# Embedding products on a shared PSUM bank, the last token tiles, a partition maximum and the last stores: a hybrid encoder block on one core

## Chip, cores and metric

One core of one Trainium2 chip runs the whole program in one launch. The metric is the device time in microseconds (us) of that core; a profiled execution gives a span, from its first to its last instruction, and a trace. PE is TensorE, DVE VectorE, ACT ScalarE, POOL GpSimd, SP the engine whose queue issues most DMAs.

## What is computed

Two sequences (a prompt and a sample) of 2048 tokens with 1024 channels go through one encoder layer with shared weights:

```
z = rmsnorm(h) @ w_in                  # q | k | v | gate a | f | gate f
a  = softmax(q k^T / 8) v * silu(ga)   # 8 query heads, 2 key heads, width 64, rotary positions
fo = (Re FFT2(f) per group @ w_fmix) * silu(gf)
h  = h + concat(a, fo) @ w_out
h  = h + (p @ w_ple) * sigmoid(rmsnorm(h) @ w_ple_gate)
y  = rmsnorm(h)
```

## The kernel before

Matrices are split into a high and a low float16 half, and a product of two splits is three matmuls. The program has three parts.

**Projection.** `project` forms z tile by tile and stores q and k (`qTd`, `kTd`), v, gates and the first half of the transform in DRAM. A store made in one iteration is put in the list `stores_next` and issued at the start of the next iteration; what is left is issued in the last one, `i == n + 3`.

**Attention with a filler.** `attention` runs 64 units (sequence, key head, 128 queries) of 8 steps. A step puts on the PE the scores of two key tiles (`scores`, bank `ps_s`), the maxima of a later unit (`maxima`, `ps_m`, reduced on DVE as `a_mx`), and in some steps more: at step 4 of a unit the softmax sums of the unit before (`sums`), at step 6 the row maxima (`max_rows`, called from `turn`), at steps 0 and 4 the products with v (`pv`). ACT takes exponentials from `ps_s`, POOL adds them up (`acc`). Behind each step `interleave` lets a generator, the filler, write its own instructions for a share of the total `FILL`, in us as the code counts them; a filler that yields `None` ends its share of that step. PE, ACT, DVE and SP run in the order in which this code is written; POOL's order is set by the framework's scheduler.

The filler is first `fourier2`, the second half of the transform, and from its middle on `outp`: for each of 32 token tiles t, `out1` (product with w_out, two halves of the columns), then a norm, `out3` (the gate product) and the embedding's product, six matmuls, which close the tile. `mix` finds the scale that a sequence's tiles are split with, from a maximum over all partitions. A group of 24 full matmuls is done as 24 matmuls over the upper 64 rows of the array and 24 over the lower 64; `slot` holds a group back by one slot, so that `halves` writes the lower half of one group alternately with the upper half of the next, each pair side by side on the array.

Of the eight PSUM banks, scores, maxima and outputs take five; `ps_g` has two buffers (the groups of `outp`) and `ps_f` has **one**, the small bank. While `outp` runs, `bank()` hands out `ps_f` alone: to the sums (read by DVE's reciprocal and a multiplication), the row maxima (read by DVE as `mr`), and the embedding's products (read by DVE at L1405 and L1407). `defer` puts such a DVE operation into a list that `flush` issues at the start of the next step.

**Tail.** After the last attention step the bank pool `psX` opens with five banks, and the rest of `outp` runs without the attention and in the scheduler's order. From there on `slot` takes groups whole, 24 matmuls over 128 rows. A `seen` copy on DVE stands ahead of the lower half that is left over.

Of the kernel before, what the change touches and what calls it, by code (L numbers as in the profile page):

```python
# [29 lines left out]
CAP = 5.0  # L30
FILL = 775.0
AHEAD = 13
# [7 lines left out]
LAG = 3  # L40
P32 = 7
STOPS = (6, 9, 12, 15, 18)
MB = 2
# [96 lines left out]
class Build:  # L140
    def __init__(self, ctx, tc, a, y):
        self.ctx, self.tc, self.nc = ctx, tc, tc.nc
        self.a, self.y = a, y
        nc = self.nc
        ep = ctx.enter_context
        self.const = ep(tc.tile_pool(name="const", bufs=1))
        self.st = ep(tc.tile_pool(name="st", bufs=2))
        self.psF = ep(tc.tile_pool(name="psF", bufs=1, space=PSUM))
        self.psG = ep(tc.tile_pool(name="psG", bufs=2, space=PSUM))
        self.grouped = False  # L150
# [408 lines left out]
    def project(self, P, PU, W, early, wkv, wq, wga, bg, mid):  # L559
# [163 lines left out]
        def lo_q(i):  # L723
# [19 lines left out]
            stores_next.append(lambda: nc.sync.dma_start(self.kTd[s][:, :, c].rearrange("v p y r -> p v y r"), kT[:]))  # L743

# [33 lines left out]
        def iteration(i):  # L778
# [180 lines left out]
    def fourier2(self, pool, hook):  # L959
# [135 lines left out]
    def attention(self, kvp):  # L1095
# [88 lines left out]

        def max_rows(u):

            ps = self.bank()
            nc.tensor.matmul(ps[:, 0:128], nm[:], self.ident[:], start=True, stop=True)  # L1188
            MR[u] = mr = kvp.tile([128, 4, 128], F16, name="mr", bufs=1)
            nc.vector.tensor_tensor(out=mr[:], in0=ps[:, 0:128].unsqueeze(1).to_broadcast([128, 4, 128]),  # L1190
                                    in1=own[:].unsqueeze(2).to_broadcast([128, 4, 128]), op=ALU.mult)
# [36 lines left out]

        def sums(u):

            s, kv, t = units[u]
            acc, at = ACC.pop(u), AT.pop(u)
            av = acc[:, 0, :].rearrange("p (c e q) -> p e c q", e=2, q=128)
            ps = self.bank()
            for e in range(2):
                nc.tensor.matmul(ps[64 * e:64 * e + 64, 0:256], ones[:], av[:, e], start=True, stop=True)  # L1236
            r, x = ps[:, 256:512], at[:].rearrange("p c q -> p (c q)")
            nc.vector.reciprocal(r, ps[:, 0:256])  # L1238
            nc.vector.tensor_tensor(out=x, in0=x, in1=r, op=ALU.mult)
# [25 lines left out]

        def turn(g):
            v, k = divmod(g + 2, 8)
            if k == 0 and 0 <= v < n:
                max_rows(v)

        def leads():
            for g in range(-AHEAD, 0):
                yield from lead(g)
                yield
                turn(g)

        self.ahead = leads()
        pool = yield 0.0
        ones = pool.tile([128, 64], F32, name="ones", bufs=1)
        nc.gpsimd.memset(ones[:], 1.0)  # L1280
        fresh = {last[0, kv]: kv for kv in range(2)}
        for g in range(8 * n + 7):
# [10 lines left out]
            if j == 4 and 0 <= u - 1 < n:  # L1293
                sums(u - 1)
# [4 lines left out]
            turn(g)  # L1299
            yield 0 if heavy else RATE if g >= 8 * n // 2 else 1 if g > FIRST else SLOW  # L1300


    def mix_max(self, s):
        nc, st = self.nc, self.st
        m = st.tile([128, 4], F32, name="mx4")
# [3 lines left out]
        mm = st.tile([128, 4], F32, name="mx4r")  # L1309
        nc.gpsimd.partition_all_reduce(mm[:, 0:3], m[:, 0:3], 128, bass_isa.ReduceOp.max)  # L1310
        return mm

# [10 lines left out]
    def mix(self, s, out):  # L1323

        sc = []
        yield from self.after(self.defer(lambda: sc.append(self.mix_max(s))), 1)
        yield from self.after(self.defer(lambda: out.append(self.mix_scale(s, sc[0]))))

    def outp(self, pool0, ow, open_pool):
# [60 lines left out]
        def out3(t, n):  # L1390
            hT = HT[t]

            def fin(ps):
# [4 lines left out]

                def embed():
                    pp = self.bank()  # L1400
# [8 lines left out]

                    TK[t] = self.defer(last)  # L1410

                return embed

            return (lambda b, k: hT[:, b, k, :], lambda b, k: ow[f"pg{n}"][b][:, k, :], fin)

        def slot(up):
# [6 lines left out]
            if up is not None and self.psX is None:  # L1423
# [4 lines left out]
            else:  # L1428
                if low is not None:
                    yield from halves(None, low)  # L1430
                if up is not None:
                    ps = self.group_bank()
                    yield from self.mm(ps[:], up[0], up[1])
                    more = up[2](ps)
                    if more is not None:
                        more()
                        yield 1.28

        def halves(up, low):
            i = n = 0  # L1440
            for k in range(8):
                for ia, ib in SPLIT3:
# [11 lines left out]
            if more is not None:  # L1454
                more()
                yield 1.48
            if self.dq is not None and self.nflush == n:
# [84 lines left out]
        def middle(t):  # L1542

            ss = st.tile([128, 2], F32, name="h_ss")
            if not (ok(t) and ok(t - 2)):
                nc.gpsimd.memset(ss[:], 1.0)
            if ok(t - 2):
                yield from self.after(TK[t - 2])
                square(t - 2, 1, ss)
# [29 lines left out]
        load_x(0)  # L1579
        held, started, due, tm, tk, t4 = [], [], [], [], {}, {}  # L1580
        self.grouped = True
        for t in range(N2 + 2):
            pr = prep(t + 1) if ok(t + 1) else iter(())
            if ok(t):
                yield from along(slot(out1(t, 0)), pr)
                if t == 1:
                    yield from middle(0)
                yield from along(slot(out1(t, 1)), pr)
                load_p(t)
                M.pop(t)  # L1590
            if ok(t - 1):
                yield from wait(tk, t - 1)
                yield from along(slot(out3(t - 1, 0)), pr)
            elif t:
                yield from along(slot(None), pr)
            if t:
                yield from middle(t)
            if ok(t - 1):
                yield from along(slot(out3(t - 1, 1)), pr)
            if ok(t + 1):  # L1600
# [35 lines left out]
    def run(self):  # L1636
# [92 lines left out]
        def fill():  # L1729
            self.nw2k = NW  # L1730
            C0 = fill_stack.enter_context(pool("C0", side="right"))
            with pool("B", side="right") as B:
                self.bd = B.tile([128, 2, 4, 128], F32, name="bd")
                nc.sync.dma_start(self.bd[:], self.bdd)
                ow = {}
# [92 lines left out]
```

## Time and profile before

| | |
|---|---|
| median of 3 runs | 2775.71 us (2775.57 to 2778.31) |
| the profiled execution's own time | 2775.26 us |
| its span | 2773.5 us |
| PE busy | 2656.9 us, 96% |
| POOL busy | 1636.9 us |
| DVE busy | 1684.4 us |
| ACT busy | 1214.7 us |

The time is the span and 1.76 us around it. A matmul in a row shows its own duration; two that overlap advance the PE by less than their sum. PEclk is the clock granted to the PE, as a share of full speed.

### The profile page before, as it was taken

How to read it: one execution, taken by the hardware profiler on the slowest of the kernel's cores; microseconds unless marked ns; L12 is line 12 of the kernel's file. 1: busy time of each engine (PE TensorE's matmuls, PEld its weight loads, DVE VectorE, ACT ScalarE, POOL GpSimd, SP SyncE). 2: the span in 40 equal slices, each digit the busy share in tenths (PEclk: the TensorE clock that was granted, in tenths of full speed). 3: DMA queues.
4: the chain of work that ended last, by engine and by line, in shares of the span. 5: the costliest groups of instructions: out<-in, count | busy, mean ns of one | idle time of the engine just before them, and what ended most of it. 6: DMA issues, size and time to landing. Idle time of an engine off the chain costs nothing.

```text
span 2773.5 us, 46318 instructions
## 1 busy us (share of the span) xinstructions
PE 2656.9 (96%) x18236; PEld 1264.5 (46%) x18236; DVE 1684.4 (61%) x2469; ACT 1214.7 (44%) x2047; POOL 1636.9 (59%) x1394
## 2 busy tenths in 40 slices
PE   6899999999998989999999999999999999999998
PEld 3455565655555543443444434433443344434433
DVE  6755555564564664666666766666656666666644
ACT  3443333432224543554445554444444445444541
POOL 1233224332336786777768877776677677767760
PEclk9999999999999999999999999999999999999998
DMA  7467566674428752222222223322222232222222
GB/s 231 143 192 187 175 184 180 185 179 121 129 70 238 236 169 88 56 71 54 69 56 54 69 67 82 82 62 71 56 67 60 60 82 54 67 71 64 63 73 61
DMA packets 418555, 296.74 MB, mean 107 GB/s; under 512 B 259456, under 2 KB 360000, under 8 KB 418336
## 3 DMA queue, kind: packets, MB, share of 16 engines
q1 hardware_dynamic: 405424, 252.01, 34.7%
q0 software_dynamic: 12912, 41.77, 4.2%
q8 instruction: 143, 2.34, 0.3%
q14 instruction: 76, 0.62, 0.1%
HBM read 149.50 MB, written 86.51 MB: 85 GB/s over the span
## 4 chain that ended last, share of the span: by engine, by line
PE 83%; DVE 7%; issue 3%; DMA 2%; POOL 2%; ACT 2%; SPq 0%; DVEq 0%; POOLq 0%; ACTq 0%
PE ps_g L1445 22%; PE ps_o L1202 15%; PE ps_x L444 14%; PE ps_s L1137 12%; PE ps_f L444 6%; PE ps_g L444 6%; PE ps_m L1164 3%; DVE a_mx L1172 1%; PE ps_f L1236 1%; PE ps_f L1188 1%; ACT p L1140 1%; POOL acc L1145 1%; PE ps_g L1056 1%; DVE h L1407 1%; DVE ps_f L1405 1%
## 5 line engine op out<-in xcount | busy, mean ns | idle before, releaser
L1145 POOL TENSOR_TENSOR acc<-acc,p 128x1024 f32<-128x1024 f32 x384 | 917.2, 2388 | 225.4 <-ACT p L1140 163.2
L1140 ACT ACTIVATE p<-ps_s,s_scale 128x512 f32<-128x512 f32 x1024 | 648.0, 684 | 692.9 <-PE ps_s L1137 667.4
L1172 DVE TENSOR_REDUCE a_mx<-ps_m 128x1 f32<-128x1024 f32 x499 | 610.4, 1223 | 534.6 <-PE ps_m L1164 525.6
L1445 PE MATMUL ps_g<-w_pg,hT 64*128 64x512 f16 x2832 | 507.8, 378 | 5.4 <-DVE seen L1422 3.0
L1202 PE MATMUL ps_o<-p,v 128*64 128x512 f32 x2048 | 467.0, 598 | 0.0
L1137 PE MATMUL ps_s<-q,k 64*128 64x512 f16 x3072 | 438.7, 378 | 7.6 <-ACT p L1140 7.4
L444 PEld LDWEIGHTS <-uc 128*128 128x128 f16 x3072 | 301.6, 98 | 311.3 <-issue 22.1
L1445 PEld LDWEIGHTS <-hT 64*128 64x128 f16 x2832 | 206.2, 94 | 169.4 <-issue 19.7
L1445 PE MATMUL ps_g<-w_wo,mh 64*128 64x512 f16 x1488 | 269.6, 378 | 3.6 <-DVE mh L1367 2.3
L1137 PEld LDWEIGHTS <-k 64*128 64x128 f16 x3072 | 148.8, 94 | 261.2 <-issue 140.5
L1445 PE MATMUL ps_g<-w_wo,mT 64*128 64x512 f16 x1488 | 264.5, 376 | 0.4 <-DMA mT<-mh 0.3
L1202 PEld LDWEIGHTS ps_o<-p,v 128*64 128x64 f32 x2048 | 143.8, 137 | 255.7 <-issue 247.2
L1164 PE MATMUL ps_m<-k,q 64*128 64x512 f16 x998 | 205.1, 377 | 16.6 <-DVE a_mx L1172 15.7
L1143 POOL TENSOR_TENSOR acc<-p,p 128x1024 f32<-128x1024 f32 x64 | 150.5, 2352 | 98.2 <-ACT p L1140 97.9
L444 PEld LDWEIGHTS <-w_ga 128*128 128x128 f16 x1536 | 151.5, 99 | 53.1 <-issue 22.6
L926 POOL DMA_DIRECT2D gfd<-gt x32 | 19.3, 602 | 218.1 <-DVE gt L954 213.2
L1445 PEld LDWEIGHTS <-mh 64*128 64x128 f16 x1488 | 101.7, 94 | 97.9 <-issue 17.4
L1445 PEld LDWEIGHTS <-mT 64*128 64x128 f16 x1488 | 107.2, 94 | 81.2 <-DMA mT<-mh 1.3
L1218 ACT ACTIVATE tb<-ps_o,a_scale 64x256 f32<-64x256 f32 x128 | 60.1, 469 | 164.2 <-PE ps_o L1202 163.4
L444 PE MATMUL ps_x<-uc,w_ga 128*128 128x256 f16 x1008 | 115.0, 275 | 5.1 <-ACT ge L911 4.5
L944 POOL DMA_DIRECT2D agd<-gat x64 | 35.9, 561 | 134.1 <-DVE gat L954 134.0
L1238 DVE RECIPROCAL ps_f<-ps_f 128x256 f32<-128x256 f32 x60 | 105.4, 1756 | 7.6 <-PE ps_f L1236 7.6
(317 smaller groups left out, 3365.7 us busy)
## 6 DMA issues: line engine op xcount, KB each, us to landing
q<-qTd SPq DMA_DIRECT2D x256, 64.0 KB, 2.3
ag<-agd SPq DMA_DIRECT2D x64, 256.0 KB, 3.2
out<-h POOLq DMA_DIRECT2D x31, 512.0 KB, 3.2
x<-in_x_prompt SPq DMA_DIRECT2D x16, 512.0 KB, 4.8
w_st<-in_w_out SPq DMA_DIRECT2D x32, 256.0 KB, 4.1
gfd<-gt POOLq DMA_DIRECT2D x32, 256.0 KB, 3.4
gd<-ge POOLq DMA_DIRECT2D x32, 256.0 KB, 3.7
agd<-gat POOLq DMA_DIRECT2D x64, 128.0 KB, 2.4
```

Source lines behind the costliest of these rows:

```text
L444: self.nc.tensor.matmul(ps, lhs(ia, k), rhs(ib, k), start=(i == 0), stop=(i == 3 * ks - 1))
L944: nc.gpsimd.dma_start(self.agd[s][1, r * 128:(r + 1) * 128, c * n:(c + 1) * n], gt[:, :n])
L1137: nc.tensor.matmul(S[u][e][:], w[sl], q[sl].rearrange("p h q -> p (h q)"), start=j == i == 0, stop=i + 1 == len(todo), skip_group_check=True)
L1140: nc.scalar.activation(p[:, e, :], S[u][e][:], AF.Exp, scale=self.sc["s_scale"][:])
L1143: nc.gpsimd.tensor_tensor(out=ACC[u][:], in0=P[u, 0][:], in1=p[:], op=ALU.add)
L1145: nc.gpsimd.tensor_tensor(out=ACC[u][:], in0=ACC[u][:], in1=p[:], op=ALU.add)
L1164: nc.tensor.matmul(ps[c], Q[u][0][sl, h, :], kt[s, kv, half][sl, :, 0, :], start=True, stop=True)
L1172: nc.vector.reduce_max(MX[u][:, h, half, c:c + 1], x, axis=AX.X)
L1202: nc.tensor.matmul(o[64 * e:64 * e + 64, :], vt[s, kv, c // 8][:, c % 8, :], p[:, e, :], start=(j == 0), stop=(j == 7))
L1218: nc.scalar.activation(tb[64 * e:64 * e + 64], ov[64 - 64 * e:128 - 64 * e, e], AF.Copy, scale=self.sc["a_scale"][64 - 64 * e:128 - 64 * e ...
L1238: nc.vector.reciprocal(r, ps[:, 0:256])
L1445: nc.tensor.matmul(g[0][:], g[1](ia, k)[sl], g[2](ib, k)[sl], start=a, stop=z, skip_group_check=True)
```

## The change

1. **Embedding's products.** At the end of an `out3` group they are no longer written at once, but put in a list `todo`. A new generator `embed` takes them out when the attention step is 1, 2 or 7 of its unit, and otherwise in the second half of the next group (`i >= 12`), or when `middle` needs the tile. Before the end of a group the code waits (`after(ticket)`) until the deferred DVE operations of the last products have been issued; each such wait yields `None`.
2. **Whole groups** from tile 30 on (`WHOLE`), instead of from the end of attention on. `FILL` is 765 instead of 775.
3. **Partition maximum.** `mix` asked POOL for `partition_all_reduce`. It now transposes the three maxima by a matmul with the identity, reduces on DVE, spreads the result over a diagonal and sums it to all partitions with two matmuls by ones.
4. **Loads and stores.** `bd` and `c2x` are loaded behind the first tile's loads of `fourier2`, not ahead of them. `last_stores` becomes GpSimd's queue in the last iteration of `project`.

`max_rows`, `sums` and `divide` are rearranged in the code, at the same steps.

```diff
-FILL = 775.0
+FILL = 765.0
+WHOLE = 2 * NT - 2
...
-                stores_next.append(lambda t=t, qT=qT: nc.sync.dma_start(self.qTd[s][t], qT[:]))
+                stores_next.append(lambda t=t, qT=qT: self.last_stores.dma_start(self.qTd[s][t], qT[:]))
...
             if i == n + 3:
                 self.drain(bg)
                 self.drain(self.ahead)
+                self.last_stores = nc.gpsimd
                 for f in stores_next:
                     f()
...
-        nc.sync.dma_start(cx[:], self.a["c_dft2x"])
         for t in range(FP):
             loads(t)
-        while todo:
-            todo.pop(0)()
+            while todo:
+                todo.pop(0)()
+            if t == 0:
+                nc.sync.dma_start(cx[:], self.a["c_dft2x"])
+                nc.sync.dma_start(self.bd[:], self.bdd)
...
-        nc.gpsimd.partition_all_reduce(mm[:, 0:3], m[:, 0:3], 128, bass_isa.ReduceOp.max)
...
+        m = self.small.tile([128, 64], F32, name="mx4", bufs=1)
+        nc.gpsimd.memset(m[:], 0.0)
+        yield from self.after(self.defer(lambda: self.mix_max(s, m)))
+        ps = self.bank()
+        nc.tensor.matmul(ps[0:64, 0:128], m[:], self.ident[:], start=True, stop=True)
+        r, mm = [st.tile([128, 4], F32, name=f"mx4{b}", bufs=1) for b in "rs"]
+        nc.vector.memset(r[:], 0.0)
+        nc.vector.tensor_reduce(out=r[0:64, 0:1], in_=ps[0:64, 0:128], op=ALU.max, axis=AX.X)
+        nc.vector.tensor_scalar(out=m[:], in0=self.ident[:, 0:64], scalar1=r[:, 0:1], scalar2=None, op0=ALU.mult)
+        yield from self.after([self.nflush])
+        ps = self.bank()
+        for e in range(2):
+            nc.tensor.matmul(ps[64 * e:64 * e + 64, 0:64], self.ones[:], m[:], start=True, stop=True)
+        nc.vector.tensor_copy(mm[:, 0:3], ps[:, 0:3])
...
-            if low is not None and (low[4] or self.psX is not None):
+            if low is not None and (low[4] or whole):
...
+                for i, us in enumerate(self.mm(ps[:], up[0], up[1])):
+                    yield us
+                    yield from embed(i >= 4)
+                yield from self.after(ticket)
+                yield from end(up[2](ps))
+
+        def embed(now=False):
+
+            if todo and (now or self.dq is None or self.step % 8 in (1, 2, 7)):
+                todo.pop()()
+                yield 1.48
...
                     if i in STOPS:
                         yield 0.216 * (i - n)
                         n = i
+                        yield from embed(i >= 12)
+            yield from self.after(ticket)
             n = self.nflush
             more = low[3](low[0]) if low is not None else None
             yield 0.216 * (24 - STOPS[-1])
-            if more is not None:
-                more()
-                yield 1.48
+            yield from end(more)
```

The first place is DVE in unit 13, where its rows show at which step the products lie. `ps_f<-th,ps_f` and `h<-ps_f` read the products of the step before; each `a_mx` closes one attention step; `RECIPROCAL` and `at<-at,ps_f` read the sums of step 4, `mr` the row maxima of step 6. Before:

```order
L1177 TENSOR_REDUCE a_m_12478<-a_mx 128x4
L1172 TENSOR_REDUCE a_mx<-ps_m 128x1
L1405 SCALAR_TENSOR_TENSOR ps_f<-th,ps_f 128x512
L1407 SCALAR_TENSOR_TENSOR h<-ps_f,p_wp_6903,h 128x512
L1172 TENSOR_REDUCE a_mx<-ps_m 128x1
L1238 RECIPROCAL ps_f<-ps_f 128x256
L1239 TENSOR_TENSOR at<-at,ps_f 128x256
L1172 TENSOR_REDUCE a_mx<-ps_m 128x1 x2
L1190 TENSOR_TENSOR mr<-ps_f,own 128x512
```

Of the change, the same stretch:

```order
L1181 TENSOR_REDUCE a_m_12476<-a_mx 128x4
L1176 TENSOR_REDUCE a_mx<-ps_m 128x1 x2
L1244 RECIPROCAL ps_f<-ps_f 128x256
L1245 TENSOR_TENSOR at<-at,ps_f 128x256
L1176 TENSOR_REDUCE a_mx<-ps_m 128x1 x2
L1193 TENSOR_TENSOR mr<-ps_f,own 128x512
L1421 SCALAR_TENSOR_TENSOR ps_f<-th,ps_f 128x512
L1423 SCALAR_TENSOR_TENSOR h<-ps_f,p_wp_6903,h 128x512
```

The pair stood in the step of the sums, so its products were written on the PE in step 3; now it stands behind the row maxima, its products in step 6. In the whole PE order the products of 57 groups in attention stand before in steps 1, 2, 3, 5, 6 and 7 with 9, 8, 10, 12, 10 and 8 groups, and now in steps 1, 2, 5, 6 and 7 with 10, 9, 6, 10 and 21 (56 groups), none in step 3.

The second place is POOL at the first `mix`; `acc` rows are the sums of exponentials, `fo<-fo,gf_in` belongs to `fourier2`, and the two rows `ISA` without names around `mx4r` change POOL's program. Before:

```order
L1145 TENSOR_TENSOR acc<-acc,p_9611 128x1024
L1022 TENSOR_TENSOR fo<-fo,gf_in 128x512 x2
L1310 ISA
L1310 ISA mx4r<-mx_9649 128x3
L1145 ISA
L1145 TENSOR_TENSOR acc<-acc,p_9655 128x1024
L1022 TENSOR_TENSOR fo<-fo,gf_in 128x512
```

Of the change:

```order
L1149 TENSOR_TENSOR acc<-acc,p_9611 128x1024
L1024 TENSOR_TENSOR fo<-fo,gf_in 128x512 x2
L1149 TENSOR_TENSOR acc<-acc,p_9654 128x1024
L1149 TENSOR_TENSOR acc<-acc,p_9689 128x1024
L1329 MEMSET mx_14491 128x64
```

The three rows of the reduction are gone; of the new way POOL keeps a memset.

The third place is DVE where the attention ends. `RECIPROCAL` and `at<-at,ps_f` belong to the last unit, `mh<-ag` splits the last tile (it needs that unit's result back from DRAM), and `seen` is what the left-over lower half on the PE waits for. Before:

```order
L1238 RECIPROCAL ps_f<-ps_f 128x256
L1239 TENSOR_TENSOR at<-at,ps_f 128x256
L1383 SCALAR_TENSOR_TENSOR h<-ps_g,mixo_14564,h 128x512
L1367 SCALAR_TENSOR_TENSOR mh<-ag,mix_s,mh 128x1024
L1422 COPY seen<-ps_g 128x1
```

Of the change:

```order
L1244 RECIPROCAL ps_f<-ps_f 128x256
L1245 TENSOR_TENSOR at<-at,ps_f 128x256
L1439 COPY seen<-ps_g 128x1
L1421 SCALAR_TENSOR_TENSOR ps_f<-th,ps_f 128x512
L1423 SCALAR_TENSOR_TENSOR h<-ps_f,p_wp_6899,h 128x512
```

`seen` stands ahead of the split now, and tile 30 follows the attention, where before it was in it.

## Rows read from the trace of the kernel before

**Rows 1.** Page, part 1: busy us (share of span), instructions.

```profile
PE 2656.9 (96%) x18236; PEld 1264.5 (46%) x18236; DVE 1684.4 (61%) x2469; ACT 1214.7 (44%) x2047; POOL 1636.9 (59%) x1394
```

**Rows 2.** Windows: length, busy us by engine, then PEclk, DMA share, GB/s.

```profile
840.00:870.00 30.00, 21.46 (x141) 13.91 (x140) 10.40 (x16) 11.41 (x19) 10.47 (x11) 0.83 0.90 256
...
965.00:1000.00 35.00, 27.98 (x176) 15.08 (x172) 19.30 (x31) 15.13 (x25) 22.71 (x14) 0.90 0.61 189
...
1105.00:2697.00 1592.00, 1563.64 (x11660) 647.75 (x11658) 1005.58 (x1040) 778.15 (x1291) 1176.26 (x998) 1.00 0.25 65
2697.00:2764.00 67.00, 63.80 (x310) 26.78 (x306) 26.29 (x66) 12.66 (x19) 3.13 (x6) 0.92 0.28 69
```

**Rows 3.** PE's waits, 1105 to 2697 us: total us, times, longest.

```profile
PE ps_f L1236 <- DVE h L1407: 6.2, 8, 0.8
PE ps_f L444 <- DVE mr L1190: 6.0, 4, 1.5
PE ps_f L1188 <- DVE h L1407: 5.8, 9, 0.7
```

**Rows 4.** Tile ps_f, same stretch: ns min/median/max, first and last start.

```profile
L1405 DVE SCALAR_TENSOR_TENSOR ps_f<-th,ps_f x58: 679/696/697, 1124.5 to 2694.9; 128x512 f32<-128x512 f32 x58
L1407 DVE SCALAR_TENSOR_TENSOR h<-ps_f,p_wp,h x58: 751/751/752, 1125.2 to 2695.7; 128x512 f32<-128x512 f32 x58
```

**Rows 5.** Timeline, POOL at the first partition maximum: start us, us, [idle before].

```profile
960.44 2.51 POOL L1022 TENSOR_TENSOR fo<-fo,gf_in 128x512 f32<-128x512 f32 x2
968.95 0.38 POOL L1310 PARTITION_ALL_REDUCE mx4r<-mx  x1 [5.99 <-issue]
977.51 2.35 POOL L1145 TENSOR_TENSOR acc<-acc,p 128x1024 f32<-128x1024 f32 x1 [8.18 <-issue]
```

**Rows 6.** Timeline, PE and DVE from 966 to 988 us.

```profile
966.07 3.65 PE L1202 MATMUL ps_o<-p,v 128*64 128x512 f32 x16
...
981.12 1.42 DVE L1020 TENSOR_TENSOR fo<-ps_g,fo 128x512 f32<-128x512 f32 x2 [4.40 <-POOL fo L1022]
...
986.52 0.61 PE L1164 MATMUL ps_m<-k,q 64*128 64x512 f16 x2 [5.58 <-DVE a_mx L1172]
...
987.97 5.89 PE L1202 MATMUL ps_o<-p,v 128*64 128x512 f32 x16
```

**Rows 7.** Windows at the second partition maximum, columns as in rows 2.

```profile
1438.00:1468.00 30.00, 29.18 (x227) 12.35 (x225) 19.76 (x31) 15.43 (x26) 16.91 (x9) 1.00 0.14 40
```

**Rows 8.** Timeline, SP's queue and PE before `fourier2` starts.

```profile
853.96 0.39 SPq L1734 DMA_DIRECT2D bd<-bdd  x1
...
854.92 0.37 SPq L979 DMA_DIRECT2D c<-in_c_dft  x1
...
859.76 3.50 PE L1056 MATMUL ps_g<-c,g_in 128*128 128x128 f32 x16 [5.22 <-DMA g_in<-gd]
```

**Rows 9.** Timeline, DVE and PE after the attention's end.

```profile
2709.16 1.28 DVE L1367 SCALAR_TENSOR_TENSOR mh<-ag,mix_s,mh 128x1024 f16<-128x1024 f32 x1 [7.55 <-ACT mh L1362]
...
2710.36 0.15 DVE L1422 COPY seen<-ps_g 128x1 f32<-128x1 f32 x1
...
2710.57 8.16 PE L1445 MATMUL ps_g<-w_pg,hT 64*128 64x512 f16 x24 [2.96 <-DVE seen L1422]
...
2757.12 5.34 PE L444 MATMUL ps_x<-w_pg,hT 128*128 128x512 f16 x24
2762.30 1.46 PE L444 MATMUL ps_g<-wp,pT 128*128 128x512 f16 x6
```

**Rows 10.** Timeline, PE in a step without filler.

```profile
846.60 0.37 PE L1137 MATMUL ps_s<-q,k 64*128 64x512 f16 x1 [0.54 <-ACT p L1140]
847.17 0.80 PE L1137 MATMUL ps_s<-q,k 64*128 64x512 f16 x5 [0.21 <-ACT p L1140]
```

**Rows 11.** Timeline, PE: row maxima and products with lone half groups.

```profile
1030.86 0.49 PE L1188 MATMUL ps_g<-ident,nm 128*128 128x128 f32 x2
...
1040.69 2.75 PE L1445 MATMUL ps_g<-w_wo,mh 64*128 64x512 f16 x12
```

More of the change, by code (lines that the diff above doesn't have):

```diff
@@ L742, in lo_q @@
                                         ks[:].rearrange("p v y t d -> p (v y t d)"))
-            stores_next.append(lambda: nc.sync.dma_start(self.kTd[s][:, :, c].rearrange("v p y r -> p v y r"), kT[:]))
+            stores_next.append(lambda: self.last_stores.dma_start(self.kTd[s][:, :, c].rearrange("v p y r -> p v y r"), kT[:]))
         def sweep_part(us):
@@ L1227, in gather, with sums, divide @@
             self.defer(lambda: self.defer(add))
-        def sums(u):
-            s, kv, t = units[u]
[L1232 to L1238, printed above, removed]
+        def sums(u, ps):
+            acc = ACC.pop(u)
+            av = acc[:, 0, :].rearrange("p (c e q) -> p e c q", e=2, q=128)
+            for e in range(2):
+                nc.tensor.matmul(ps[64 * e:64 * e + 64], self.ones[:], av[:, e], start=True, stop=True)
+        def divide(u, r):
+            s, kv, t = units[u]
+            at = AT.pop(u)
+            x = at[:].rearrange("p c q -> p (c q)")
+            nc.vector.reciprocal(r, r)
             nc.vector.tensor_tensor(out=x, in0=x, in1=r, op=ALU.mult)
@@ L1274, in leads @@
                 yield
-                turn(g)
+                if g == -2:
+                    max_rows(0, self.bank()[:, 0:128])
         self.ahead = leads()
         pool = yield 0.0
-        ones = pool.tile([128, 64], F32, name="ones", bufs=1)
-        nc.gpsimd.memset(ones[:], 1.0)
+        self.ones = pool.tile([128, 64], F32, name="ones", bufs=1)
+        nc.gpsimd.memset(self.ones[:], 1.0)
         fresh = {last[0, kv]: kv for kv in range(2)}
@@ L1298, in attention, with mix_max @@
                 pv((g - 1) // 8, (g - 1) % 8 - PVG + 1)
-            turn(g)
+            if j == 6 and u + 1 < n:
+                max_rows(u + 1, self.bank()[:, 0:128])
             yield 0 if heavy else RATE if g >= 8 * n // 2 else 1 if g > FIRST else SLOW
-    def mix_max(self, s):
-        nc, st = self.nc, self.st
-        m = st.tile([128, 4], F32, name="mx4")
+    def mix_max(self, s, m):
+        nc = self.nc
         nc.vector.tensor_reduce(out=m[:, 0:1], in_=self.tmax[s][:], op=ALU.max, axis=AX.X)
@@ L1323, in mix @@
     def mix(self, s, out):
-        sc = []
-        yield from self.after(self.defer(lambda: sc.append(self.mix_max(s))), 1)
-        yield from self.after(self.defer(lambda: out.append(self.mix_scale(s, sc[0]))))
+        nc, st = self.nc, self.st
+        m = self.small.tile([128, 64], F32, name="mx4", bufs=1)
[8 more added lines that the diff above has]
+        yield from self.after([self.nflush])
+        ps = self.bank()
+        for e in range(2):
+            nc.tensor.matmul(ps[64 * e:64 * e + 64, 0:64], self.ones[:], m[:], start=True, stop=True)
+        nc.vector.tensor_copy(mm[:, 0:3], ps[:, 0:3])
+        yield None
+        yield from self.after(self.defer(lambda: out.append(self.mix_scale(s, mm))))
     def outp(self, pool0, ow, open_pool):
@@ L1397, in fin, with products @@
                 x, h = X[t], self.sc[f"p_wp{n}"][:, t:t + 1]
[L1399 removed]
+                def products():
                     pp = self.bank()
@@ L1408, in last, with slot @@
                                                        op0=ALU.mult, op1=ALU.add)
-                    TK[t] = self.defer(last)
-                return embed
+                    nonlocal ticket
+                    ticket = TK[t] = self.defer(last)
+                return products
             return (lambda b, k: hT[:, b, k, :], lambda b, k: ow[f"pg{n}"][b][:, k, :], fin)
-        def slot(up):
+        def slot(up, whole):
             low = held.pop() if held else None
-            if low is not None and (low[4] or self.psX is not None):
+            if low is not None and (low[4] or whole):
                 j = st.tile([128, 1], F32, name="seen")
                 nc.vector.tensor_copy(j[:], low[0][:, 0:1])
-            if up is not None and self.psX is None:
+            if up is not None and not whole:
                 up = (self.group_bank(), *up, not started)
@@ L1427, in slot, with end @@
                 yield from halves(up, low)
[L1428 to L1434, printed above, removed]
-                    if more is not None:
-                        more()
-                        yield 1.28
+                return
+            if low is not None:
+                yield from halves(None, low)
+            if up is not None:
+                ps = self.group_bank()
+                for i, us in enumerate(self.mm(ps[:], up[0], up[1])):
[7 more added lines that the diff above has]
+                yield 1.48
+        def end(more):
+            if more is not None:
+                todo.append(more)
+                yield from embed()
         def halves(up, low):
@@ L1547, in middle @@
             if ok(t - 2):
+                yield from embed(True)
                 yield from self.after(TK[t - 2])
@@ L1579, in outp @@
         load_x(0)
-        held, started, due, tm, tk, t4 = [], [], [], [], {}, {}
+        ticket = [-1]
+        todo, held, started, due, tm, tk, t4 = [], [], [], [], [], {}, {}
         self.grouped = True
@@ L1584, in outp @@
             if ok(t):
-                yield from along(slot(out1(t, 0)), pr)
+                yield from along(slot(out1(t, 0), t >= WHOLE), pr)
                 if t == 1:
                     yield from middle(0)
-                yield from along(slot(out1(t, 1)), pr)
+                yield from along(slot(out1(t, 1), t >= WHOLE), pr)
                 load_p(t)
@@ L1592, in outp @@
                 yield from wait(tk, t - 1)
-                yield from along(slot(out3(t - 1, 0)), pr)
-            elif t:
-                yield from along(slot(None), pr)
+                yield from along(slot(out3(t - 1, 0), t >= WHOLE), pr)
             if t:
@@ L1598, in outp @@
             if ok(t - 1):
-                yield from along(slot(out3(t - 1, 1)), pr)
+                yield from along(slot(out3(t - 1, 1), t >= WHOLE), pr)
             if ok(t + 1):
@@ L1730, in fill @@
             self.nw2k = NW
-            C0 = fill_stack.enter_context(pool("C0", side="right"))
+            self.small = C0 = fill_stack.enter_context(pool("C0", side="right"))
             with pool("B", side="right") as B:
                 self.bd = B.tile([128, 2, 4, 128], F32, name="bd")
-                nc.sync.dma_start(self.bd[:], self.bdd)
                 ow = {}
```

20 lines of the change are left out of this document (6 added, 14 removed).

## Prediction

> **What bounds the kernel now.** The page's busy shares come first: the PE is busy for 2656.9 of 2773.5 us [rows 1], so the end moves with the 116.6 us in which it is idle and with the time in which it runs at a lower granted clock; another engine counts only where the PE waits for it. A table of windows by stage shows where [rows 2]. What the change touches lies in four places. (a) The start of `fourier2`: 8.5 us idle in 840 to 870, clock 0.83. (b) The stretch from 965 to 1000: 7.0 idle, clock 0.90. (c) The long attention with `outp`: 28.4 idle in 1592 us, full clock. (d) The tail from 2697: 3.2 idle, clock 0.92. Next I read who ends the PE's waits in each, and the timeline around the longest. The sum is made against the profiled execution: its own time, 2775.26 us, is its span and 1.76, and 0.45 below the median of the runs. Under 0.2%, 5.5 us, a difference cannot be told from none.
>
> **The products, stage (c).** Nearly two thirds of the idle time is waits for the one small bank, 18.0 us in 21 waits [rows 3]. Each kind belongs to a step. Products written in step 3 are read by DVE at the start of step 4 (0.70 + 0.75 us [rows 4]), and the sums wait for that: 8 waits, 6.2 us. Products of step 5 make the row maxima of step 6 wait: 9 waits, 5.8 us. Products written right behind the row maxima wait for `mr`: 4 waits, 6.0 us.
>
> The order fences and the counts beside them price what is left. Step 3 has no products any more, for 10 groups before: minus 6.2. Step 5 has 6, for 12: if as many of them wait as before (9 of 12, 0.64 us each), 2.9 are left of 5.8. Step 6 still has 10; I counted in the PE order of the change that 3 stand directly behind the row maxima (4 before) at 1.5 us, and 2 behind a piece of six matmuls, some 0.65 us of cover, so 0.85 each: 6.2 for 6.0. The sum is minus 8.9. I add minus 1, since in the order 4 of the attention steps from 64 to 500 have under 1.3 us of work beside their scores, where before there were 6, four of them with nothing but maxima. So **minus 10**. Bounds: nothing, if the waits only move, and minus 18 if all go. The 21 groups that now stand in step 7 are read by DVE in step 0, where `pv` alone keeps the PE busy for 3.65 us [rows 6] against 1.45 of DVE: that is the cover. With it gone, each of the 13 groups that step 7 has more would cost up to 1.45.
>
> The wait for `ticket` before a group's end holds back, in the filler, `fin`'s DVE or ACT operation and all later filler of that step; scores and maxima of the next step don't stand behind it. It costs the PE only if a step is left with scores and maxima alone: then the next scores wait 0.54 + 0.21 us for the exponentials [rows 10].
>
> **The partition maximum, stage (b).** POOL stands still for 5.99 us before `partition_all_reduce`, works 0.38, and stands still for 8.18 after it [rows 5]: 14.6 us, in which it should have done six `acc`. What is late next: POOL's products `fo`, for which DVE waits 4.40; behind that DVE's `a_mx`, for which the PE waits 5.58; then the clock falls, and the same 16 matmuls of `pv` take 5.89 us for 3.65 [rows 6]. Idle 7.0 and the clock's share, 27.98 x 0.10 = 2.8, make 9.8 us in this window; some 0.8 of idle is usual for 35 us in this kernel (28.4 in 1592 is 0.6), so **minus 9**. The second reduction, near 1446, cost nothing: in the 30 us around it the PE is idle for 0.8 [rows 7], since POOL's backlog there meets seven buffers of exponentials. So nothing is won there.
>
> Added instead, twice: three small matmuls, a few short DVE operations, and a memset on POOL. The nearest row for the PE is the row maxima's product, same shape, 0.49 us for its pair [rows 11]; three at 0.25 are 0.75, **plus 1.5** for both, and up to 3 if the PE waits for DVE in between. The transposition stands behind the step's scores and maxima, while DVE does three reductions of under 0.2 us, and the two products stand a step later.
>
> Here the Trainium skill, "GPSIMD Engine Reference", section 4.1, speaks against the change: a reduction along partitions is GpSimd's, it says, and by that the change would lose its plus 1.5 and win nothing. Section 2.1 says that the first call of freshly loaded code costs GpSimd about 6 us that no instruction shows; the 5.99 in this trace agree, but the 8.18 behind it aren't in it, and by the page alone the stall would be 6.4 us, not 14.6.
>
> **The tail, stage (d).** Before, the left-over lower half waited 2.96 us for `seen`, which stood on DVE behind the split of the last tile, and this behind the last unit's way through DRAM [rows 9]. In that pause the clock fell: 24 lone half matmuls took 8.16 us, where 12 had taken 2.75 [rows 11], and the next six took 2.74 for 1.46 [rows 9]. All in all the stage holds 63.80 x 0.92 = 58.7 us of work in 67.0: 8.3 lost. In the order of the change `seen` stands ahead of the split, and between the last sums and tile 31 the PE has tile 30's two whole groups, a lone half, two groups of tile 29 and four sets of products: 4 x 5.34 + 5.34 + 4 x 1.46 = 32 us (at the rates of [rows 9]), where the split of tile 31 ended 13.4 us into this stage. **Minus 8.** A whole group takes 5.34 [rows 9], 0.22 a matmul, and the code counts 0.216 for a pair of halves, so `WHOLE` itself is nothing. The lower `FILL` moves 10 us of work, as the code counts, from attention into the tail; that is free if attention is bound by the PE, as stage (c) says, and plus 10 if it isn't at all.
>
> **Loads and stores, stage (a).** The PE waits 5.22 us for the first `g_in` [rows 8]. `c` is issued 0.96 us earlier without `bd` and `c2x` ahead, and `bd`'s 512 KB no longer share the way: at 256 GB/s [rows 2] up to 2 us. `bd` is first needed about 5 us after `g_in`, its cover. Bounds 0 and minus 3; **minus 2**. The stores do **not** move: those of the last chunk are issued at the start of iteration `n + 3`, and `last_stores` changes at its end. In the order SP still issues the same qTd and kTd stores ahead of q, and POOL none. So that part is worth nothing.
>
> The sum: -10 - 9 + 1.5 - 8 - 2 = -27.5, and 2775.26 - 27.5 is **2748 us**.
>
> **The rivals.**
> - *The bank waits only move.* For it: DVE reads the products wherever they stand. Against: the waits belong to steps in which another user of the bank follows at once, and step 7 has none behind it until step 1. Then (c) gives 0: 2758.
> - *The partition maximum was hidden, or the new one is as long.* For it: the second one was. Against: the chain POOL, DVE, PE is seen at the first. Then (b) gives 0 and the plus 3: 2758.
> - *DVE's step 0 becomes the wait.* The 13 groups more in step 7 cost 1.45 each, 18.9, and (c) wins nothing: 2748 + 10 + 18.9 = 2777, no change. Against: DVE is busy for 63% of stage (c).
> - *Slower: the wait for `ticket` empties steps.* Place: the end of 62 of the groups in attention. If each left a step with scores and maxima alone, 0.75 us each, it would be plus 46: 2794. It turns the sign from 37 such steps on. Against: the order shows no such growth.
>
> **Chances.** The forecast 0.66, its own range 2739 to 2757; the bank 0.12; the maximum 0.10; DVE's step 0 0.06; empty steps 0.06. With the low bounds, -18 - 9 + 1.5 - 8 - 3, it would be 2739; if `FILL` cost its 10 on top of either of the next two cases, 2768. The range takes in the three of them up to half of that: 2738 to 2764. Faster is the first three, 0.88; no change 0.06; slower 0.06.
>
> **What would show it.** After: PE waits for ps_f near 9 us, with none of the sums for `h`; no POOL gap over 5 us in 960 to 980 and no clock under 1 there; the wait for `g_in` near 3 us; no `seen` wait and full clock from the last attention step to the last products, with a longer tail; stores still on SP. It would be wrong if waits of `ps_m` for `a_mx` or of `ps_s` for `p` grew by over 10 us in the long stage, or if the tail's extra work met an attention that isn't shorter.

## The result and the profile after

The changed kernel takes **2747.49 us** (median of 4, 2743.69 to 2747.83) against 2776.89 before on the same chip: ratio 0.9891, 95% interval 0.9874 to 0.9908. The forecast was 2748. In the profiled executions the span fell from 2773.5 to 2746.0, by 27.5 us, which is the sum of the forecast to the tenth; by stage it is not the forecast's sum, and the experiments show that two of its terms do not stand by themselves. Differences of whole times below are taken from the ratios, as a share of the 2779 us that the kernel before takes.

Page, part 1, of the changed kernel; then windows for those of [rows 2], the third from the first product with hT to the last scores, the fourth from there to the last product:

```profile
PE 2649.2 (96%) x18176; PEld 1261.7 (46%) x18176; DVE 1702.8 (62%) x2477; ACT 1213.0 (44%) x2047; POOL 1631.3 (59%) x1394
```
```profile
840.00:870.00 30.00, 22.59 (x152) 15.66 (x151) 11.17 (x17) 11.55 (x20) 11.55 (x11) 0.89 0.88 254
965.00:1000.00 35.00, 35.00 (x250) 19.99 (x245) 27.70 (x40) 20.98 (x35) 31.78 (x20) 1.00 0.87 273
1086.74:2656.39 1569.65, 1545.43 (x11516) 638.43 (x11516) 1011.58 (x1036) 770.84 (x1281) 1163.67 (x978) 1.00 0.25 66
2656.39:2736.29 79.90, 79.90 (x404) 34.69 (x400) 32.87 (x74) 20.00 (x30) 12.48 (x27) 1.00 0.32 72
```

The PE is busy in all of the stretch of the first maximum (28 of 35 before) and in all of the tail, both at full clock. In the attention 24.2 us are idle. Its waits there:

```profile
PE ps_m L1168 <- DVE a_mx L1176: 6.1, 9, 1.2
PE ps_f L445 <- DVE mr L1193: 6.0, 5, 1.5
PE ps_g L1473 <- DMA hT<-h_hl: 5.7, 1, 5.7
PE ps_f L1191 <- DVE h L1423: 4.0, 6, 0.7
PE ps_s L1141 <- ACT p L1144: 2.0, 9, 0.3
```

Against [rows 3] the waits of the sums for `h` are gone, those of the row maxima are 4.0 us for 5.8, those of the products for `mr` 6.0 for 6.0: the bank costs 10.0 us for 18.0. Nobody forecast the 5.7 us for hT.

**Maximum.** POOL, then PE and DVE, where [rows 5] and [rows 6] stood:

```profile
962.49 4.81 POOL L1149 TENSOR_TENSOR acc<-acc,p 128x1024 f32<-128x1024 f32 x2
967.23 0.16 POOL L1329 MEMSET mx<- 128x64 f32 x1
```
```profile
960.63 0.43 PE L1332 MATMUL ps_g<-ident,mx 128*64 128x128 f32 x2
...
963.05 0.34 PE L1340 MATMUL ps_g<-mx,ones 128*64 128x64 f32 x4
...
965.59 3.65 PE L1205 MATMUL ps_o<-p,v 128*64 128x512 f32 x16
...
961.70 0.89 DVE L1336 TENSOR_SCALAR mx<-ident,mx4r 128x64 f32<-128x64 f32 x1
```

Instead of 14.6 us of POOL the maximum costs the PE 0.43 + 0.34 us, 1.5 for both times, and DVE 1.4 us the first time and 1.9 the second.

**Loads.** SP and PE, for [rows 8]:

```profile
854.48 0.39 SPq L981 DMA_DIRECT2D c<-in_c_dft  x1
...
856.43 0.42 SPq L1045 DMA_DIRECT2D bd<-bdd  x1
...
857.81 3.75 PE L1060 MATMUL ps_g<-c,g_in 128*128 128x128 f32 x16 [2.77 <-DMA g_in<-gd]
```

**Tail.** DVE and PE, for [rows 9]: `seen` follows the last sums at once, and no wait stands before the lone half, whose first 12 matmuls take 2.76 us (24 took 8.16).

```profile
2670.61 0.15 DVE L1439 COPY seen<-ps_g 128x1 f32<-128x1 f32 x1
...
2671.05 2.76 PE L1473 MATMUL ps_g<-w_pg,hT 64*128 64x512 f16 x12
```

**The new wait.** SP, DVE and PE at the start of `outp`:

```profile
1082.99 1.23 SPq L1524 DMA_TRANSPOSE hT<-h_hl  x1
...
1087.57 1.20 SPq L1379 DMA_TRANSPOSE mT<-mh  x1
1089.77 1.23 SPq L1529 DMA_TRANSPOSE hT<-h_hl  x1
...
1084.40 3.14 DVE L1383 SCALAR_TENSOR_TENSOR mh<-ag,mix_s,mh 128x1024 f16<-128x1024 f32 x1
1087.47 2.28 DVE L1527 SCALAR_TENSOR_TENSOR h_hl<-h,h_r,h_hl 128x1024 f16<-128x1024 f32 x1
...
1093.09 0.60 PE L1473 MATMUL ps_g<-w_pg,hT 64*128 64x512 f16 x1 [5.75 <-DMA hT<-h_hl]
```

The split `mh` of the next tile stands ahead of `h_hl`'s second half on DVE, and `mT` ahead of `hT` on SP; before, both stood behind. A matmul behind the wait takes 0.60 us where its kind takes 0.39: the granted clock is 0.50 from 1092 to 1097 us. That alone is not new, since behind the 2.2 us wait before the first matmuls were slow too; then 8 pairs were, now 12.

**Stages.** Each kernel's profiled span, cut at the start of the first product with `g_in`, of the first `out1`, of the first product with hT, at the last scores and the last product (in us; another 9.7 to 10.0 follow), and its timed ratio to before on its own chip. One execution stands behind each row, and that of before (2775.26) is at the low end of its runs on those chips (2775 to 2783, medians 2778.8 to 2779.8), so small differences of one stage say little.

| kernel | to g_in | fourier2 | to hT | attention | tail | ratio, 95% |
|---|---|---|---|---|---|---|
| before | 859.8 | 180.9 | 58.5 | 1586.7 | 77.9 | 1 |
| changed | 857.8 | 171.5 | 57.4 | 1569.7 | 79.9 | 0.9891, 0.9874 to 0.9908 |
| e1, maximum alone | 859.7 | 171.2 | 58.5 | 1587.3 | 79.6 | 0.9958, 0.9943 to 0.9973 |
| e2, products put off alone | 859.0 | 182.7 | 59.6 | 1589.2 | 81.9 | 1.002, 1.001 to 1.0029 |
| e3, WHOLE and FILL alone | 855.2 | 180.7 | 57.4 | 1580.7 | 84.3 | 0.9966, 0.9955 to 0.9976 |
| e4, loads alone | 857.2 | 181.7 | 58.5 | 1587.6 | 77.8 | 0.9993, 0.9984 to 1.0003 |
| f1, changed, products back | 858.5 | 170.5 | 57.0 | 1579.2 | 81.0 | 0.9935, 0.9921 to 0.995 |
| f2, changed, FILL 775 | 858.8 | 171.8 | 58.7 | 1590.5 | 70.1 | 0.9933, 0.9917 to 0.995 |
| f3, changed, FILL 770 | 859.9 | 172.8 | 61.2 | 1567.4 | 75.8 | 0.9893, 0.9879 to 0.9908 |
| f4, changed, stores moved | 854.5 | 171.6 | 57.1 | 1570.1 | 79.9 | 0.9882, 0.9867 to 0.9896 |
| g1, FILL alone | 861.9 | 180.4 | 56.9 | 1579.1 | 85.1 | 0.9969, 0.9956 to 0.9981 |
| g2, WHOLE alone | 860.8 | 182.3 | 59.7 | 1585.3 | 69.2 | 0.9965, 0.9952 to 0.9978 |
| g3, changed, last piece | 858.0 | 170.6 | 57.0 | 1566.6 | 79.9 | 0.9868, 0.9853 to 0.9882 |
| g4, all mended | 854.9 | 171.6 | 59.6 | 1555.8 | 77.4 | 0.9832, 0.9817 to 0.9846 |

### The profile page after: what moved, and what is told of

Its sections match the earlier page's. It is cut to its first block, busy times and chain, and to the rows that moved or that the text cites. A ratio compares the mean times of both kernels' runs of the same rounds, so it can differ in the third digit from the quotient of the medians.

```text
span 2746.0 us, 46196 instructions
## 1 busy us (share of the span) xinstructions
PE 2649.2 (96%) x18176; PEld 1261.7 (46%) x18176; DVE 1702.8 (62%) x2477; ACT 1213.0 (44%) x2047; POOL 1631.3 (59%) x1394
## 4 chain that ended last, share of the span: by engine, by line
PE 86%; DVE 6%; issue 2%; DMA 2%; ACT 1%; POOL 1%; SPq 0%; DVEq 0%; ACTq 0%; POOLq 0%
PE ps_g L1473 22%; PE ps_o L1205 16%; PE ps_x L445 15%; PE ps_s L1141 13%; PE ps_f L445 6%; PE ps_g L445 6%; PE ps_m L1168 4%; PE ps_f L1237 1%; DVE a_mx L1176 1%; PE ps_f L1191 1%; PE ps_g L1012 1%; PE ps_g L1060 1%; DVE w_mx L312 1%; ACT p L1144 0%; PE ps_x L911 0%
## 5 line engine op out<-in xcount | busy, mean ns | idle before, releaser
L1473 PE MATMUL ps_g<-w_pg,hT 64*128 64x512 f16 x2784 | 494.8, 377 | 5.8 <-DMA hT<-h_hl 5.7
L1473 PEld LDWEIGHTS <-hT 64*128 64x128 f16 x2784 | 200.2, 94 | 165.3 <-issue 20.7
L1473 PE MATMUL ps_g<-w_wo,mh 64*128 64x512 f16 x1440 | 261.6, 378 | 1.4 <-DVE seen L1439 1.4
L1473 PE MATMUL ps_g<-w_wo,mT 64*128 64x512 f16 x1440 | 256.7, 377 | 0.6 <-DMA mT<-mh 0.6
L1473 PEld LDWEIGHTS <-mT 64*128 64x128 f16 x1440 | 100.6, 94 | 84.6 <-issue 2.3
```

The source lines that it names most:

```text
L1473: nc.tensor.matmul(g[0][:], g[1](ia, k)[sl], g[2](ib, k)[sl], start=a, stop=z, skip_group_check=True)
```

## The experiments

The theory is that of the prediction: each part of the change takes its own wait away, and the terms add. The rivals are its rivals, and one that came up with the single runs: the parts work on each other through the filler's pace.

**e1.** Before, with `mix` and `mix_max` of the change.

```diff
-        nc.gpsimd.partition_all_reduce(mm[:, 0:3], m[:, 0:3], 128, bass_isa.ReduceOp.max)
...
+        nc.tensor.matmul(ps[0:64, 0:128], m[:], self.ident[:], start=True, stop=True)
```

> Before, with the partition maximum by transposition alone (mix, mix_max, and the pool and the ones that they use). Theory, by the prediction's step (b): 9 us won at the first maximum and 1.5 spent on both, so -7.5, near 2768 us, ratio 0.9973; PE idle for under 1.5 us from 965 to 1000 at a clock of 1, and no POOL gap over 5 us there. Rival, the maximum was hidden or the new one is as long: 0 to +3, 2775 to 2778, with as much idle time in that stretch as before, 7.0 us, only with other releasers.

Measured 2767.83 us, ratio 0.9958: -11.7 us, interval -16 to -8. `fourier2` is 9.7 us shorter, the PE busy for 35.00 of 35.00 us from 965 to 1000. The theory stands; that the reduction was hidden does not. In the table `fourier2` is 170.5 to 172.8 us in all eight kernels with the new maximum and 180.4 to 182.7 in the six without it.

**e2.** Before, with `todo`, `embed` and `ticket` alone.

```diff
...
-            if more is not None:
-                more()
-                yield 1.48
+            yield from end(more)
```

> Before, with the products put off alone (todo, embed, ticket); whole groups from the end of attention on as before, FILL 775, partition_all_reduce as before. Theory, by step (c): -10, near 2765 us, ratio 0.9964; waits of the PE for ps_f in the long attention 18.0 us before, now 9 to 10, none of them of the sums for h. Rival, the bank waits only move: 2775, 18 us of ps_f waits behind other steps. Rival, DVE's step 0 becomes the wait: up to 2794, waits of ps_m for a_mx up by over 10 us.

Measured 2783.94, ratio 1.002: slower by 5.6, and outside both what the theory and what "they only move" expected. The waits of its attention:

```profile
PE ps_f L444 <- DVE mr L1190: 8.2, 8, 1.5
PE ps_s L1137 <- ACT p L1140: 6.8, 17, 1.1
PE ps_g L1457 <- DVE mh L1367: 6.3, 8, 1.4
PE ps_f L1188 <- DVE h L1407: 4.8, 7, 0.9
PE ps_m L1164 <- DVE a_mx L1172: 3.7, 10, 0.7
```

The bank waits fell to 13.0, but the waits for `mh`, `p` and `a_mx` rose, over the same stretch, from 2.3, 4.7 and 2.4 to 6.3, 6.8 and 3.7. That is 2.4 more, and the attention is 2.5 us longer. But the profiled span is 8.6 longer than before: the tail has 4.0 of it, where `seen` is waited for 3.4 us (3.0 before) and the 24 lone halves behind it take 10.40 us (8.16 before).

**e3, g1, g2.** Before, with both of `WHOLE` and `FILL`, and with each by itself.

```diff
-FILL = 775.0
+FILL = 765.0
...
+WHOLE = 2 * NT - 2
```

> Before, with whole groups from tile 30 on and FILL 765 alone. Theory, by step (d): -8 in the tail, no wait for seen, clock 1 there. The trace of the changed kernel shows one thing that the prediction did not name: at the start of outp the PE waits 5.75 us for the first hT, against 2.2 before, and its clock falls. In the order of this kernel SP has the transposition of mT ahead of the second half of hT, as in the changed one, where before it stands behind; so if FILL is what shifts it, this kernel shows it too, some +2 to +3: net -5 to -6, 2769 to 2770, ratio 0.998. If the hT wait is instead a matter of the maximum or of the products, it stays at 2 us here and the whole is -8, 2767. Rival, the tail's extra work is not hidden: +2 or more.

> Before with FILL 765 alone. In its order seen stands ahead of the last split, as in the changed kernel. By the prediction's step (d), FILL moves 10 us into the tail for nothing and takes the seen wait away: -8, 2769. If the tail's gain needs whole groups (lone halves run at half the rate), the tail grows by the 10 us and more, the attention shrinks by 6 (as in the run with whole groups and FILL): 2775 or more.

> Before with whole groups from tile 30 on alone, FILL 775. The prediction held WHOLE itself for nothing: 2775. With the products put off and FILL 775 the tail went from 81.9 to 70.1 us when whole groups came with it: by that -8 to -10, tail near 69, no wait for seen, clock 1: 2766 to 2768.

Measured 2770.67 (0.9966), 2771.61 (0.9969) and 2768.9 (0.9965): each alone gives what both give, -8.6 to -9.7. With `WHOLE` alone the tail is 69.2 us, 8.7 shorter, and the PE is busy in all of it:

```profile
2688.16:2757.39 69.23, 69.23 (x320) 30.12 (x318) 34.02 (x70) 16.79 (x25) 10.42 (x10) 1.00 0.36 82
```

So at FILL 775 `WHOLE` alone gives the tail's 8. With `FILL` alone `seen` isn't waited for either, but a wait of 3.3 us for hT stands in the tail instead; the tail grows by 7.2 and the attention shrinks by 7.6 in the profiled execution (own time 2775.0, the slowest of its six, 2767.07 to 2775.02), so where its 8 come from isn't seen there. Nor is it with both: attention and tail together are 1665.0 us for 1664.6 before, and what e3's profiled execution has won lies ahead of `fourier2` (4.6) and before hT (1.1). What `WHOLE` adds at FILL 765 is therefore open: no run leaves it out of the changed kernel. Both kernels with FILL 765 wait 5.5 us for the first hT, g2 1.5: the late hT is FILL's.

**e4.** Before, with `c2x` and `bd` loaded behind the first tile's loads.

> Before, with bd and c2x loaded behind the first tile's loads alone. Theory, by step (a): -2 (bounds 0 and -3), 2773.3, ratio 0.9993; the PE's wait for the first g_in near 3 us for 5.2. Rival, the DMA way is full either way: the wait for g_in shrinks and another one (q, or the second g_in) grows by as much, 2775.

Measured 2777.3, ratio 0.9993, interval 0.9984 to 1.0003: the wait for `g_in` is 2.9 us for 5.2, as forecast, but the whole can't be told from nothing.

**f1.** The changed kernel with the products written at once again (the reverse of e2's edit).

> The changed kernel with the products written at once again (todo, embed and ticket undone; maximum, whole groups, FILL 765 and loads as changed). Prediction's step (c): +10 over the changed kernel, 2757. What the single runs suggest: with FILL 775 the bank waits fell by 5 only and other waits grew, with FILL 765 and the products at once the bank waits are 22.9 us for 10.0 in the changed kernel, so here +13: 2760, ps_f waits near 23. If the products put off are worth nothing, as alone: 2747 to 2750.

Measured 2761.69, ratio 0.9935 to 0.9891 for the changed kernel: putting off is worth 12 us here (0.0044 of 2779), give or take 6, where the prediction had 10. Attention and tail together take 1660.2 us for 1649.6. The PE is idle for 35.3 us in the attention, 22.9 of them bank waits.

**f2, f3.** The changed kernel with FILL 775 and 770.

> The changed kernel with FILL 775 again. By the prediction FILL is free, 10 us between attention and tail: 2747.5, within 2. Other theory, from the run with the products put off alone: at 775 the filler comes to a tile's products before its split mh is there, and steps are left without filler: waits for mh and for p together up by 5 to 9 us against the changed kernel, the first hT wait back at 2 (-4), seen behind the split again (+3 and its clock): 2752 to 2756.

> The changed kernel with FILL 770. In the order SP has the first hT's second half ahead of the next mT again, as before the change, and seen stands ahead of the last sums and of the last split. If the late hT is what the changed kernel loses at the start of outp: the hT wait 2 us for 5.7 and full clock there, -5, 2742 to 2743, unless mh and p waits appear as at 775 (then 2747 or more).

At 775 2761.02 (0.9933): 12 us slower, give or take 7. The tail is as good as in g2, and the attention idles for 32.5 us. One place of it, PE and DVE:

```profile
2020.19 0.57 PE L1168 MATMUL ps_m<-k,q 64*128 64x512 f16 x2
2021.25 0.37 PE L1141 MATMUL ps_s<-q,k 64*128 64x512 f16 x1 [0.49 <-ACT p L1144]
2021.83 0.80 PE L1141 MATMUL ps_s<-q,k 64*128 64x512 f16 x5 [0.21 <-ACT p L1144]
...
2028.79 0.39 PE L1473 MATMUL ps_g<-w_wo,mh 64*128 64x512 f16 x1 [1.38 <-DVE mh L1383]
...
2026.16 2.57 DVE L1383 SCALAR_TENSOR_TENSOR mh<-ag,mix_s,mh 128x1024 f16<-128x1024 f32 x1
```

The same steps in the kernel before:

```profile
2029.62 1.47 PE L444 MATMUL ps_f<-wp,pT 128*128 128x512 f16 x6
...
2032.84 0.65 PE L1236 MATMUL ps_f<-acc,ones 128*64 128x256 f32 x4 [0.77 <-DVE h L1407]
...
2037.71 0.39 PE L1445 MATMUL ps_g<-w_wo,mh 64*128 64x512 f16 x1 [0.25 <-DVE mh L1367]
...
2035.87 1.79 DVE L1367 SCALAR_TENSOR_TENSOR mh<-ag,mix_s,mh 128x1024 f16<-128x1024 f32 x1
```

Before, the six products are all that fills step 3: the filler has nothing else, since the next tile's split is still to come. They cost the sums 0.77. Put off, they leave the step with scores and maxima alone (0.49 + 0.21), the next group waits 1.13 us longer for `mh` (0.78 of it is the split itself, 2.57 us here for 1.79), and the products' 1.47 still come, in step 5. This is what the rival "the wait for `ticket` empties steps" names, though the putting off does it here and not the wait, and it happens at two tiles only (here and at 2404 us): the other pairs of waits for `p` in the attention of f2 stand in the kernel before as well, and in all they are 5.4 us for 4.7.

The larger part is `mh`: 8 waits, 6.2 us, for 4 and 2.3 before. Four tiles wait that did not, at 1113, 1523, 1969 and 2411 us. The second of them, f2 first, then before:

```profile
1523.03 0.39 PE L1473 MATMUL ps_g<-w_wo,mh 64*128 64x512 f16 x1 [1.12 <-DVE mh L1383]
...
1519.79 3.18 DVE L1383 SCALAR_TENSOR_TENSOR mh<-ag,mix_s,mh 128x1024 f16<-128x1024 f32 x1
```
```profile
1531.28 1.47 PE L444 MATMUL ps_f<-wp,pT 128*128 128x512 f16 x6
...
1529.66 3.19 DVE L1367 SCALAR_TENSOR_TENSOR mh<-ag,mix_s,mh 128x1024 f16<-128x1024 f32 x1
```

The split lasts as long as before, but before the six products stood ahead of the new tile's group and covered its last 1.5 us. At 770 the waits for `mh` and `p` are 2.3 and 2.9, at 765 none and 2.0: at that pace no group comes ahead of its split. That the pace does it is shown, most plainly by f2 against f3 on the same chip, 2761.0 us for 2749.4 at a FILL that differs by 5; why so small a step is enough was not followed further.

At 770 the kernel takes 2749.36 (0.9893), the same as changed: hT's wait is back at 1.2 us and attention and tail are 6.4 shorter together, but 3.8 are lost between the first `out1` and hT. There the clock fell twice, at 1056 and at 1086 us, behind small gaps. Windows of f3, then of f2, at the same steps, the stretch ahead and the stretch itself:

```profile
1051.00:1056.00 5.00, 4.20 (x33) 1.89 (x30) 4.21 (x5) 4.22 (x7) 3.49 (x2) 1.00 0.15 30
1056.00:1061.00 5.00, 4.79 (x18) 1.50 (x19) 3.03 (x3) 1.77 (x3) 4.83 (x3) 0.66 0.60 180
```
```profile
1049.00:1054.00 5.00, 4.21 (x32) 1.88 (x29) 4.17 (x5) 4.18 (x7) 3.45 (x2) 1.00 0.16 32
1054.00:1059.00 5.00, 4.78 (x26) 1.58 (x25) 3.75 (x3) 1.81 (x3) 4.84 (x3) 1.00 0.62 178
```

**f4.** The changed kernel with `last_stores` set where the stores are still to be issued.

```diff
             stores, stores_next = stores_next, []
+            if i == n + 3:
+                self.last_stores = nc.gpsimd
...
-                self.last_stores = nc.gpsimd
```

> The changed kernel with last_stores set at the start of the last iteration, so that the last qTd and kTd stores really go to GpSimd's queue. If SP's queue is what holds q and g_in back there: SP is free of 4.7 us of issues and waits, the waits for q (1.7) and g_in (2.8) fall, up to -4, 2743.5. Rival: in the order POOL has these two stores ahead of the last gd and agd stores, and they wait there for the transpositions as they did on SP; g_in is read from gd, so it comes no earlier or later: 2747 to 2750.

Measured 2746.34 (0.9882): within the intervals of the changed kernel. But the place shows it. SP, POOL and PE:

```profile
850.87 0.34 SPq L982 DMA_DIRECT2D c<-in_c_dft  x1
...
842.13 0.54 POOL L740 DMA_DIRECT2D qTd<-qT  x1 [6.51 <-DMA qT<-qs]
...
846.44 0.54 POOL L915 DMA_DIRECT2D gd<-ge  x1
...
854.49 3.75 PE L1061 MATMUL ps_g<-c,g_in 128*128 128x128 f32 x16 [3.80 <-DMA g_in<-gd]
```

`c` is issued 3.6 us earlier and `fourier2` starts 3.3 earlier. The rival had the place right and not the size: `gd` is issued 3.8 us later, behind the two stores, and that was early enough. The two kernels with this edit start `fourier2` at 854.5 and 854.9, the six with the new loads and without it at 857.2 to 859.9; one execution of the old loads, e3's, lies at 855.2 too.

**g3, g4.** The changed kernel with the products forced at the last piece only; and that with the stores moved and FILL 768.

```diff
-                        yield from embed(i >= 12)
+                        yield from embed(i >= 18)
```

> The changed kernel with put-off products forced only at the last of the pieces of the next group (i >= 18 for 12). In the order the groups in step 5 fall from 6 to 1 and in step 6 from 10 to 8, step 7 has 28 for 21. If the bank waits follow the steps: waits of the row maxima for h 4.0 us to about 0.7, of products for mr 6.0 as before with 3 directly behind the row maxima; -3, 2744 to 2745. Rival, the wait for ticket now holds back the group's end and fin more often: waits of ps_s for p up from 2.0 by as much, 2747 to 2750.

> The changed kernel with the last stores really on GpSimd, FILL 768 (SP has both halves of the first hT ahead of the next mT) and the products forced at the last piece only (2 groups in step 5, 6 in step 6 of which 1 directly behind the row maxima). If the three losses named are real and add: hT wait 5.7 to 2 us (-4), bank waits 10 to 4 (-6), stores -2: 2736, ratio 0.985. If FILL 768 brings the waits for mh and p of 770 (5.2 for 2.0): 2739. If it is no faster than the changed kernel, 2747, the waits only move.

g3 takes 2743.79 (0.9868, its interval overlapping the changed kernel's): the row maxima wait 0.7 us for `h`, for 4.0, and `p` is at 2.2, so no step was emptied. g4 takes **2731.94 us**, ratio 0.9832 (0.9817 to 0.9846), faster than both kernels and 4 us below the 2736 that the three repairs were to add up to. Its waits in the attention:

```profile
PE ps_f L445 <- DVE mr L1194: 3.0, 3, 1.5
PE ps_g L1474 <- DMA hT<-h_hl: 1.5, 1, 1.5
PE ps_f L1192 <- DVE h L1424: 1.5, 2, 0.8
PE ps_g L1474 <- DVE mh L1384: 1.4, 2, 0.8
PE ps_s L1142 <- ACT p L1145: 1.2, 4, 0.6
```

11.2 us are idle in the attention (1555.83 less 1544.64 busy), for 24.2.

## Why the prediction was right, and where it was not

The total was right; two steps behind it were not, and what they left out cancelled, so that the sum came out to the tenth is luck. The terms do not add: the runs with one part each (e1 to e4) win 0.0042, lose 0.0020, win 0.0034 and win 0.0007, together 0.0063, and the change wins 0.0109.

- **(b) Maximum, -9 and +1.5.** Right in mechanism and size: `fourier2` is 9.4 us shorter in the changed kernel, 9.7 in e1, for 8.3 forecast (9 less half of the +1.5). The +1.5 is 2 x 0.77 from the rows. The page of the Trainium skill that gives such a reduction to GpSimd ("GPSIMD Engine Reference", section 4.1) would have let 0.9958 be 1 or more; e1 decides against it here.
- **(c) Products, -10.** The bank waits came out near the forecast: none of products in step 3, 4.0 us for those of step 5 (2.9 forecast), 6.0 for those of step 6 (6.2 forecast). All idle time of the attention fell by 6.3, from 30.5 to 24.2. What failed is that the term stands by itself. Putting off costs 5.6 us at FILL 775 (e2; of the 8.6 in its profiled execution 2.5 are the attention's) and wins 12 at 765 (f1). The prediction had no term for `mh`: that the products themselves had covered the next tile's split was left out. The step that said that a ticket wait "costs the PE only if a step is left with scores and maxima alone", and that the order shows no such growth, looked only at the wait for `ticket`; at 775 two steps are left short by the putting off itself. The count of short steps was made at FILL 765, where it holds.
- **(d) Tail, -8.** Right in size: no `seen` wait, full clock, 79.9 of 79.9 busy. Wrong in part in cause: "so `WHOLE` itself is nothing". At FILL 775 `WHOLE` alone takes 8.7 off the tail (g2); at 765, where `seen` comes early without it (g1), its part is open. And that the lower `FILL` "is free if attention is bound by the PE" failed in both directions: it delays the first hT by 3.5 us, and 12 pairs of matmuls behind it are slow where 8 were, and it is what makes the put-off products pay; taking it back costs 12 us (f2).
- **(a) Loads, -2.** The wait for `g_in` fell from 5.2 to 2.8, as forecast; e4's interval still holds zero. That the stores don't move was right, and f4 shows 3.3 us at that place where they do.
- **The sum.** Attention and tail together are 15.1 us shorter, 17.3 forecast with the second half of the +1.5; `fourier2` and the way to hT 10.5 shorter, 8.3 forecast; the start 1.9, 2 forecast. In the attention the bank waits fell by 8.0, `mh` and `p` by 5.0; hT and `a_mx` took back 3.5 and 3.7, for which the prediction had no term.

The rival "the bank waits only move" fell in the changed kernel (f1) and holds nearly at FILL 775, where other waits grew by 7.4 for 5.0 won. "DVE's step 0" fell: `p` and `a_mx` together are 8.1 for 7.1, with 21 groups in step 7. Most of the growth of `a_mx` comes with FILL 765 (4.1 us in f1 and 5.0 in g1, where the products are written at once), and in g4, with the put-off products too, both waits together are 2.2.

## What to carry to other kernels

Work that makes another wait may itself be cover: the only filler of a step, or the time in which a later input gets ready. Before it is moved, look at what is left in the step that it leaves and at what comes next there, tile by tile, and not only at the bank that it frees. A number that sets a pace is not free because it only moves work past a boundary; it shifts every phase, and each edit beside it must be measured at the pace that it will run at. An order of instructions that shows no change for an edit (the stores) is worth mending: with the products' last piece and a FILL of 768 it gave another half of what the change had given.

## What the runs showed of the hardware

The cost of `partition_all_reduce` is not its 0.38 us but the two times around it in which POOL stands still: 5.99 and 8.18 us at the first maximum, 5.79 and 6.89 at the second, near 1446 us of the kernel before. Without it (e1) POOL's largest gap between 960 and 990 us is 1.92 us. At the second the PE was idle for 0.8 us of 30 ([rows 7]); taking the first away made `fourier2` 9.7 us shorter.

The same small gaps of the PE can cost the clock or not. In f3 and f2 the stretch ahead holds the same steps with 4.20 and 4.21 us busy of 5 at full clock; in the next 5 us the granted clock is 0.66 in the one, where 18 matmuls fit, and 1.00 in the other, with 26. What tells them apart no row here shows. Behind the first wait for hT the matmuls were slow (0.63 us for 0.38) in all six profiled executions that waited 5.5 to 5.8 us, in none of the four that waited 1.2 to 1.5, and in three of the four that waited 2.0 to 2.2.
